# First sublayer's modulation on one core: its weights loaded ahead of x, its rows transposed tile by tile

## The chip, the cores and the metric

The program runs on one core of a Trainium2 chip. The metric is device time in microseconds (us) of one execution; the kernel before has 2074.36 us, the median of 3 runs.

## The reference, cut to what matters

The network takes x (256 rows of 1024, fp32) through two sublayers with stick-breaking attention or retention, each followed by a sublayer with a mixture of experts, and then through a second block. The change touches what stands ahead of attention (i = 0) and of retention (i = 1):

```python
def adaln_params(c, w, b):
    m = jax.nn.silu(c) @ w + b
    shift, scale, gate = jnp.split(m, 3, axis=-1)
    return shift[:, None, :], scale[:, None, :], gate[:, None, :]

for i in range(DEPTH):
    shift, scale, gate = adaln_params(c, ada_w[i, 0], ada_b[i, 0])
    h = x * (1.0 + scale) + shift
    y = stick_breaking_attention(h, sb_w_in) if i == 0 else retention(h, positions, ret_w_in, ...)
    x = layer_norm(DEEPNORM_ALPHA * x + (1.0 + gate) * y, ln_g[i, 0], ln_b[i, 0])
    ...                     # the mixture-of-experts sublayer
```

Here `ada_w[i, 0]` is 1024 x 3072, so shift, scale and gate need 4 MB of weights each.

## The kernel before, in words

Rows of x lie in two tiles of 128 (t = 0, 1), columns in eight blocks of 128 (k = 0 to 7). Every fp32 matrix is split into a high and a low part (`split`, L148: ScalarE casts the high part, L151, VectorE subtracts it for the low part, L153 or in four pieces L160), and a product is three matmuls (`mm3`).

**Shift, scale, gate.** `ada_all` (L232) is a generator. It calls `ada_rows` (L206) for shift, scale and gate in turn; each loads four chunks of 1 MB (L217, "w<-ada_w" in the profile) and multiplies each with the repeated silu(c) in 8 matmuls of 32 x 256 (L163, "y<-w,c_rep", two records apiece in the trace). It yields behind each chunk, so that a chunk is issued where the caller asks for the next one. After scale, `ada_cols` (L241) turns the two rows into columns sc and sh, which the modulation needs; the gate comes later, its chunks between those of the projections.

**Modulation.** `modulated` (L370) wants h transposed: for each k, `transposed` (L357) takes a bank of PSUM, transposes the block of both tiles into it (L187), and calls `each`: one engine, VectorE for even k (L379), ScalarE for odd k (L377), evicts it with scale and shift into a tile t2, and `split` makes the high and low part, "a" in the profile. `modulated` runs twice: ahead of attention (source x) and of retention (source the output of the layer norm).

**Projections.** `proj_t` and `proj_n` multiply h with 256 columns of weights, 1 MB, loaded by `wload` (L385; L392 is its DMA) and split into two tiles "hl": 48 matmuls of 128 x 256 for a projection. Attention has 12 of them (sb_w_in), retention 24 (ret_w_in).

**Order.** `block1` (L1717) sets the program order: silu(c), the load of x, the constants (`consts1`), then the generators. The order on each engine is then made by a scheduler that simulates a timeline; within an `issue_after` block an instruction must come behind a named one of its engine. Pools bound what can be under way: 6 tiles w and 6 tiles hl for weights, 4 banks ps for products and transposes, 4 banks y for accumulators. All the large loads go through SP's one queue, in its order; an SP instruction that waits for a free tile holds those behind it.

Of the kernel before, what the change touches and what calls it, by code (L numbers as in the profile page):

```python
# [8 lines left out]
F32 = mybir.dt.float32  # L9
# [5 lines left out]
AF = mybir.ActivationFunctionType  # L15
# [4 lines left out]
P = 128  # L20
S = 256
T = 2
D = 1024
KB = 8
# [30 lines left out]
class Net:  # L55
    def __init__(self, ctx, tc, io, dbg=None):
        self.ctx, self.tc, self.nc, self.io = ctx, tc, tc.nc, io
        self.dbg = dbg or {}
        self.flip = self.pieces = self.wide = 0
        self.left, self.early, self.done = [], {}, {}  # L60

    def phase(self, name):
# [136 lines left out]
    def ada_init(self):  # L199
        nc = self.nc  # L200
        sc = self.cst.tile([P, KB], F32, name="c_silu")
        nc.scalar.activation(sc, self.c_col, AF.Silu)
        self.crep = self.cst.tile([P, KB, 32], F32, name="c_rep")
        nc.vector.tensor_copy(self.crep, sc[:, :, None].to_broadcast([P, KB, 32]))

    def ada_rows(self, i, j, slot, out):  # L206

        nc = self.nc
        W = self.io["ada_w"][i, j].rearrange("(k p) n -> p k n", p=P)
        if slot == 2:  # L210
            bias = self.wk.tile([P, 256], F32, name="ada_b", bufs=1)
            nc.gpsimd.dma_start(bias, self.io["ada_gate_b"][i * 2 + j])
        pm = self.acc.tile([P, 512], F32, name="y")[:, :256]
        for k2 in range(4):
            w = self.hl(F32) if self.wide > k2 % 3 else self.w()
            w = w.rearrange("p (k n) -> p k n", k=2)
            nc.sync.dma_start(w, W[:, k2 * 2:k2 * 2 + 2, slot * D:(slot + 1) * D])  # L217
            for k in range(2):
                kk = k2 * 2 + k
                for c in range(4):  # L220
                    self.mm(pm[32 * c:32 * c + 32], self.crep[:, kk, :],
                            w[:, k, c * 256:(c + 1) * 256], kk == 0, kk == 7)
            if k2 < 3:
                yield
        if slot == 2:
            nc.vector.tensor_tensor(out, pm, bias, op=OP.add)
        else:
            nc.vector.tensor_copy(out, pm)
# [75 lines left out]
    def layer_norm(self, x, y, i, j):  # L304
# [32 lines left out]
            self.left = [(t, s, x, grow, brow) for t in range(T) for s in (slice(0, 512), slice(512, D))]  # L337
        return xh

    def behind(self):  # L340

        return self.tc.issue_after(next(i for i in reversed(self.nc.cur_bb.bb.instructions)
                                        if i.engine == self.vector))
# [25 lines left out]
    def modulated(self, src, sc, sh):  # L369
        nc = self.nc  # L370
        hi, lo = (self.act8(F32R).rearrange("p (k s) -> p k s", k=KB) for _ in range(2))
        self.pieces = PC[0]

        def each(k, pt):
            f = self.t2(S)
            if k % 2:
                nc.scalar.activation(f, pt, AF.Identity, scale=sc[:, k:k + 1], bias=sh[:, k:k + 1])  # L377
            else:
                nc.vector.tensor_scalar(f, pt, sc[:, k:k + 1], sh[:, k:k + 1], op0=OP.mult, op1=OP.add)  # L379
            self.split(hi[:, k], lo[:, k], f)  # L380
        self.transposed(src, each)
        return hi, lo


# [1306 lines left out]
def consts1(net):  # L1691
    nc = net.nc
    k1 = net.load_const("pack1")
    pick(k1, PACK1, net)
    for n, v in (("nones", -1.0), ("ones", 1.0)):
        t = net.cst.tile([P, P], F32, name="c_" + n)
        nc.gpsimd.memset(t, v)
        setattr(net, n, t)
    net.zerob = net.cst.tile([P, P], BF, name="c_zerob")
    nc.gpsimd.memset(net.zerob, 0.0)  # L1700
    net.identb = net.cst.tile([P, P], BF, name="c_identb")
    nc.gpsimd.tensor_copy(net.identb, net.ident)
    net.maskb = net.cst.tile([P, P], BF, name="c_maskb")
    nc.gpsimd.tensor_scalar(net.maskb, net.stri, BIG, -BIG, op0=OP.mult, op1=OP.add)
# [13 lines left out]
def block1(net, s5=True):  # L1718
    nc = net.nc
    net.xm = net.side_pool("xm")  # L1720
    x = net.x_mid = net.xm.__enter__().tile([P, T, D], F32, name="x_mid")
    with ExitStack() as ctx:
        net.open_stream(ctx, 6, 6, 5, 6, 8, "1")
        net.phase("start")
        net.ada_init()
        nc.sync.dma_start(x, net.io["x"].rearrange("(t p) d -> p t d", p=P))
        consts1(net)
        prev = {(0, 0): None}
        for i, j in ((0, 1), (1, 0), (1, 1)):
            q = i * 2 + j - 1  # L1730
            prev[i, j] = net.lng[:, q], net.lnb[:, q]
        ada = {ij: net.ada_all(*ij, prev[ij]) for ij in prev}

        def without_gate(ij):
            while ij not in net.mod:
                yield next(ada[ij])
        net.early[0] = [net.io["ret_w_in"][0]]
        net.jobs += [ada[0, 0]] + [net.s5_params()] * s5 + [ada[0, 1], without_gate((1, 0))]
        s5 = [net.s5_tables()] * s5
        while (0, 0) not in net.mod:  # L1740
            net.background()
        src = x
        for i in range(2):
            for j in range(2):
                net.phase(f"sub{i}{j}")
                net.rate = 1
                if (i, j) == (0, 1):
                    net.rope_tables()
                if (i, j) == (1, 0):
                    net.jobs += [[ada[1, 0], ada[1, 1]] + s5, [ada[1, 0]] + s5 + [ada[1, 1]], [ada[1, 1]] + s5 + [ada[1, 0]], s5 + [ada[1, 0], ada[1, 1]]][GO]  # L1750
                sc, sh, m2 = net.mod[i, j]
                if j == 0:
                    hx = net.modulated(src, sc, sh)
                    y = net.stick(hx) if i == 0 else net.retention(hx, src)
                else:
                    y = net.moe(i, src, sc, sh)
                net.phase(f"ln{i}{j}")
                while net.jobs:
                    net.background()
                if j == 0:  # L1760
                    net.router(*net.mod[i, 1][:2])
                src = net.layer_norm(x, y, i, j)
                net.dump(f"x{i}{j}", x)
# [92 lines left out]
@with_exitstack  # L1856
def whole(ctx, tc, io):
    net = Net(ctx, tc, io)
    net.open_main(ctx)
    block1(net)  # L1860
    block2(net, io["out"])
# [16 lines left out]
```

## Time and profile before

| what | value |
|---|---|
| runs | 2067.89, 2074.36, 2075.95 us; median 2074.36 |
| profiled execution | 2072.57 us, its span 2070.8 us |
| PE (matmul) busy | 1958.4 us, 95% of the span |
| VectorE (DVE) busy | 1206.9 us, 58% |
| ScalarE (ACT) busy | 802.1 us, 39% |
| GpSimd (POOL) busy | 410.5 us, 20% |
| moved by DMA | 496.09 MB, mean 240 GB/s |

A share of busy time is a mean over stages with different limits. Attention lies at about 34 to 200 us of the span, the first mixture of experts at 205 to 456, retention at 470 to 665, and so on. A time with an interval in a row is a start and a length in us; "<-" in brackets names what ended the wait ahead of it.

### The profile page before, as it was taken

The numbers are of one execution on the slowest core, as the hardware profiler recorded it, in microseconds if no ns is written. First come the engines' busy times: TensorE is split into PE (matmuls) and PEld (weight loads), VectorE is DVE, ScalarE is ACT, GpSimd is POOL, SyncE is SP. The second block draws the span as 40 slices with busy tenths as digits, with TensorE's granted clock in tenths as the row PEclk, the third lists the DMA queues.
The fourth block names the chain that finished last, engine by engine and source line by source line (L and its number), as shares of the span: only waits on it lengthen the run. The fifth ranks groups of instructions, "written<-read, shape, count | busy, mean of one in ns | idle before, by whom it ended". The sixth has DMA issues, their size and how long they took to land.

```text
span 2070.8 us, 31874 instructions
## 1 busy us (share of the span) xinstructions
PE 1958.4 (95%) x12566; PEld 1527.3 (74%) x12567; DVE 1206.9 (58%) x2489; ACT 802.1 (39%) x1254; POOL 410.5 (20%) x319
## 2 busy tenths in 40 slices
PE   6999999989999999987988999999999999999998
PEld 4967543438898844434766889999999998888886
DVE  3554321129895422104687569767999986555555
ACT  3344111124454311113433553555444445444444
POOL 1000000002232000000231134544665550000000
PEclk9999899999999999998998999999999999999999
DMA  9797699998875699996332361544564446555564
GB/s 388 284 405 269 253 393 394 394 390 284 304 271 187 245 365 394 395 391 263 138 116 88 114 257 32 163 143 143 163 194 154 145 151 193 193 194 193 194 194 151
DMA packets 155887, 496.09 MB, mean 240 GB/s; under 512 B 10176, under 2 KB 10592, under 8 KB 147152
## 3 DMA queue, kind: packets, MB, share of 16 engines
q1 hardware_dynamic: 152880, 483.42, 65.1%
q0 software_dynamic: 2848, 10.53, 1.4%
q8 instruction: 102, 1.67, 0.3%
q14 instruction: 57, 0.47, 0.1%
HBM read 486.30 MB, written 7.61 MB: 239 GB/s over the span
## 4 chain that ended last, share of the span: by engine, by line
PE 72%; DVE 10%; ACT 2%; issue 2%; DMA 2%; POOL 1%; POOLq 0%; SPq 0%; DVEq 0%; ACTq 0%
PE ps L163 42%; PE y L163 28%; DMA w<-moe_w_down 1%; DVE pair L1553 1%; PE y L1206 1%; DVE i L1454 1%; PE ps L187 1%; DVE et L1477 1%; DVE hl L153 1%; DVE pos L1465 1%; DVE v L1453 1%; ACT hl L151 0%; DMA raw<-s_tab 0%; DVE big L1561 0%; DVE cand L1460 0%
## 5 line engine op out<-in xcount | busy, mean ns | idle before, releaser
L163 PE MATMUL ps<-hn,pair 128*128 128x256 f32 x3072 | 383.5, 285 | 4.2 <-DVE pair L1553 4.1
L163 PEld LDWEIGHTS ps<-hn,pair 128*128 128x128 f32 x3072 | 373.8, 192 | 5.6 <-DVE pair L1553 5.1
L163 PE MATMUL y<-pair,hn 128*128 128x512 f32 x1512 | 342.9, 389 | 0.0
L163 PEld LDWEIGHTS y<-pair,hn 128*128 128x128 f32 x1512 | 283.8, 188 | 59.0
L163 PE MATMUL ps<-w,t 128*64 128x512 f32 x624 | 277.3, 595 | 8.7 <-DMA w<-moe_w_down 2.8
L163 PE MATMUL ps<-hl,t 128*64 128x512 f32 x624 | 278.4, 596 | 4.5 <-DVE t L194 3.1
L1553 POOL TENSOR_TENSOR pair<-raw,pair 128x640 fp32r<-128x640 f32 x128 | 235.2, 1845 | 158.0 <-ACT pair L1551 151.8
L153 DVE TENSOR_TENSOR pair<-raw,pair 128x1024 fp32r<-128x1024 f32 x128 | 156.7, 1225 | 147.1 <-ACT pair L151 147.1
L151 ACT CAST hl<-w 128x2048 fp32r<-128x2048 f32 x79 | 150.2, 1903 | 136.6 <-PE ps L163 77.1
L151 ACT CAST pair<-raw 128x1024 fp32r<-128x1024 f32 x128 | 135.0, 1055 | 172.7 <-PE y L163 171.6
L163 PEld LDWEIGHTS ps<-w,t 128*64 128x64 f32 x624 | 81.6, 137 | 117.2 <-issue 103.8
L1551 ACT CAST pair<-raw 128x1024 fp32r<-128x1024 f32 x128 | 134.2, 1051 | 65.7 <-PE ps L163 23.9
L153 DVE TENSOR_TENSOR hl<-w,hl 128x2048 fp32r<-128x2048 f32 x51 | 119.2, 2337 | 54.2 <-ACT hl L151 51.1
L163 PE MATMUL ps<-hl,a 128*128 128x256 f32 x1008 | 129.7, 287 | 1.8 <-ACT hl L151 1.8
L163 PEld LDWEIGHTS ps<-hl,t 128*64 128x64 f32 x624 | 81.1, 137 | 67.6 <-issue 60.7
L163 PEld LDWEIGHTS ps<-hl,a 128*128 128x128 f32 x1008 | 123.9, 191 | 5.7 <-ACT hl L151 2.0
L330 POOL TENSOR_TENSOR ln_st<-ln_st,c_mhalf 128x1 f32<-128x1 f32 x8 | 6.1, 768 | 605.3 <-ACT ln_st L327 605.2
L731 DVE TENSOR_TENSOR t<-t,ps 128x512 f32<-128x512 f32 x16 | 11.0, 688 | 171.8 <-PE ps L163 171.8
L163 PE MATMUL ps<-a,hl 128*128 128x256 f32 x864 | 105.7, 284 | 1.2 <-DVE a L153 1.2
L163 PEld LDWEIGHTS ps<-a,hl 128*128 128x128 f32 x864 | 104.2, 192 | 2.6 <-DVE a L153 1.4
L163 PE MATMUL ps<-a,t 128*64 128x512 f32 (+1 forms) x352 | 100.2, 537 | 1.4 <-ACT t L196 1.4
L747 DVE SCALAR_TENSOR_TENSOR t<-ps,m_sw,t 128x512 fp32r<-128x512 f32 x32 | 24.0, 750 | 132.5 <-ACT t L746 132.0
(431 smaller groups left out, 2886.5 us busy)
## 6 DMA issues: line engine op xcount, KB each, us to landing
raw<-peer_u SPq DMA_DIRECT2D x128, 512.0 KB, 3.4
raw<-peer_v SPq DMA_DIRECT2D x128, 512.0 KB, 3.4
w<-ada_w SPq DMA_DIRECT2D x35, 1024.0 KB, 7.5
w<-moe_w_down SPq DMA_DIRECT2D x28, 1024.0 KB, 14.3
hl<-moe_w_down SPq DMA_DIRECT2D x28, 1024.0 KB, 14.2
w<-moe_w_up SPq DMA_DIRECT2D x26, 1024.0 KB, 14.2
hl<-moe_w_up SPq DMA_DIRECT2D x26, 1024.0 KB, 14.3
w<-moe_w_gate SPq DMA_DIRECT2D x24, 1024.0 KB, 14.7
```

The lines of the kernel that those rows point to most:

```text
L151: nc.scalar.copy(hi, src)
L153: nc.vector.tensor_tensor(lo, src, hi.bitcast(F32), op=OP.subtract)
L163: self.last_mm = self.nc.tensor.matmul(out, lhsT=lhsT, rhs=rhs, start=start, stop=stop, skip_group_check=True)
L187: self.nc.tensor.transpose(out, in_, self.ident[:in_.shape[0], :in_.shape[0]])
L747: V.scalar_tensor_tensor(yl[hf], py, sw, yh[hf].bitcast(F32), op0=OP.mult, op1=OP.subtract)
L1206: self.nc.tensor.matmul(py[32 * q:32 * q + 32, :S], lhsT=self.s5_ct[ct][:, 4 * i + q], rhs=ab[q % 2][:, x, ri], start=j == 0, stop=j == 3, ...
L1453: V.max(v[:, a, rs], s)
L1454: V.max_index(ix[:, a, rs], v[:, a, rs], s)
L1465: V.max_index(pos[:, 2, rs], top[:, h, rs], cd)
L1477: V.tensor_reduce(et[:, 0:2, h], oh.rearrange("p a k j -> p a j k"), axis=AX.X, op=OP.add)
L1551: nc.scalar.copy(up[:, 0], ur)
L1553: lo = eng.tensor_tensor(up[:, 1, ks], ur[:, ks], up[:, 0, ks].bitcast(F32), op=OP.subtract)
```

## The change

Two things. In `block1`, the generator for shift and scale of the first sublayer runs ahead of everything else: its first six chunks are issued, then x, then the last two chunks, then the constants. Those last two chunks take tiles of the hl pool (`self.ahead`), not of w. In `modulated`, which both places use, four banks are taken with two blocks k each; all transposes are written out tile by tile (all k of t = 0, then all of t = 1), and only then the eight calls of `each`, in each of which the instructions of VectorE and ScalarE must come behind the last ones of the call before (`in_order`).

```diff
@@ ada_rows
-            w = self.hl(F32) if self.wide > k2 % 3 else self.w()
+            w = self.hl(F32) if self.wide > k2 % 3 or self.ahead and slot == 1 and k2 > 1 else self.w()
@@
+    def in_order(self):
+
+        stack = ExitStack()
+        for eng in (self.vector, self.scalar):
+            stack.enter_context(self.tc.issue_after(next(i for i in reversed(self.nc.cur_bb.bb.instructions)
+                                                         if i.engine == eng)))
+        return stack
@@ modulated
-        self.transposed(src, each)
+        pts = [self.psum((P, 2, S)) for _ in range(KB // 2)]
+        for t in range(T):
+            for k in range(KB):
+                self.transpose(pts[k // 2][:, k % 2, t * P:t * P + P], src[:, t, k * P:k * P + P])
+        for k in range(KB):
+            with self.in_order() if k else nullcontext():
+                each(k, pts[k // 2][:, k % 2])
@@ block1
-        nc.sync.dma_start(x, net.io["x"].rearrange("(t p) d -> p t d", p=P))
+
+        net.ahead = 1
+        first = net.ada_all(0, 0, None)
+        for n in range(8):
+            if n == 6:
+                nc.sync.dma_start(x, net.io["x"].rearrange("(t p) d -> p t d", p=P))
+            next(first)
+        net.ahead = 0
         consts1(net)
-        prev = {(0, 0): None}
+        prev = {}
...
-        ada = {ij: net.ada_all(*ij, prev[ij]) for ij in prev}
+        ada = {(0, 0): first, **{ij: net.ada_all(*ij, prev[ij]) for ij in prev}}
```

The instructions stand as follows at three places. First, SP's queue at the program's start, before:

```order
L78 DMA c_pack_66<-pack 128x224
L1726 DMA x_mid<-x 128x2x1024
L217 DMA w<-ada_w 128x2x1024 x8
L392 DMA w<-sb_w_in 128x2048
L217 DMA w<-ada_w 128x2x1024
```

and now:

```order
L78 DMA c_pack_66<-pack 128x224
L217 DMA w<-ada_w 128x2x1024 x6
L1745 DMA x_mid<-x 128x2x1024
L217 DMA hl<-ada_w 128x2x1024 x2
L406 DMA w<-sb_w_in 128x2048
```

x has moved behind six of the eight chunks; what stands behind the eighth chunk is the same as before.

Second, ScalarE at the first modulation (t2 is an evicted block, a its high part, "hl<-w" the cast of a whole chunk of projection weights), before:

```order
L377 ACTIVATE t2_229<-ps_226,ada_sh_214,ada_sc_213 128x256
L151 CAST hl_281<-w_280 128x2048
L377 ACTIVATE t2_243<-ps_240,ada_sh_214,ada_sc_213 128x256
L151 CAST a_217<-t2_222 128x256
L151 CAST a_217<-t2_229 128x256
L151 CAST a_217<-t2_236 128x256
L377 ACTIVATE t2_257<-ps_254,ada_sh_214,ada_sc_213 128x256
L151 CAST a_217<-t2_250 128x256
L151 CAST a_217<-t2_264 128x256
L377 ACTIVATE t2_271<-ps_268,ada_sh_214,ada_sc_213 128x256
L151 CAST a_217<-t2_243 128x256
L151 CAST a_217<-t2_257 128x256
```

and now (w_276, w_350 and w_424 are the weights of the first three projections):

```order
L151 CAST hl_277<-w_276 128x2048
L151 CAST a_217<-t2_239 128x256
L385 ACTIVATE t2_243<-ps_219,ada_sh_202,ada_sc_201 128x256
L151 CAST a_217<-t2_243 128x256
L151 CAST a_217<-t2_247 128x256
L385 ACTIVATE t2_251<-ps_220,ada_sh_202,ada_sc_201 128x256
L151 CAST hl_351<-w_350 128x2048
L151 CAST a_217<-t2_251 128x256
L151 CAST hl_425<-w_424 128x2048
L151 CAST a_217<-t2_255 128x256
L385 ACTIVATE t2_259<-ps_221,ada_sh_202,ada_sc_201 128x256
L151 CAST a_217<-t2_259 128x256
```

The first chunk's cast has moved ahead of all blocks, and the casts of the second and third chunk have moved in front of blocks 3 and 4; before, both stood behind block 7. VectorE has the low parts of the second and third chunk at the same places between the blocks.

Third, VectorE at the second modulation, ahead of retention (L153 writes a low part), before:

```order
L379 TENSOR_SCALAR t2_3428<-ps_3425,ada_sc_1593,ada_sh_1594 128x256
L379 TENSOR_SCALAR t2_3442<-ps_3439,ada_sc_1593,ada_sh_1594 128x256
L379 TENSOR_SCALAR t2_3456<-ps_3453,ada_sc_1593,ada_sh_1594 128x256
L153 TENSOR_TENSOR a_3424<-t2_3428,a_3423 128x256
L379 TENSOR_SCALAR t2_3470<-ps_3467,ada_sc_1593,ada_sh_1594 128x256
L153 TENSOR_TENSOR a_3424<-t2_3435,a_3423 128x256
L153 TENSOR_TENSOR a_3424<-t2_3442,a_3423 128x256
```

and now:

```order
L387 TENSOR_SCALAR t2_3441<-ps_3421,ada_sc_1589,ada_sh_1590 128x256
L153 TENSOR_TENSOR a_3420<-t2_3441,a_3419 128x256
L153 TENSOR_TENSOR a_3420<-t2_3445,a_3419 128x256
L387 TENSOR_SCALAR t2_3449<-ps_3422,ada_sc_1589,ada_sh_1590 128x256
L153 TENSOR_TENSOR a_3420<-t2_3449,a_3419 128x256
L153 TENSOR_TENSOR a_3420<-t2_3453,a_3419 128x256
L387 TENSOR_SCALAR t2_3457<-ps_3423,ada_sc_1589,ada_sh_1590 128x256
L153 TENSOR_TENSOR a_3420<-t2_3457,a_3419 128x256
L153 TENSOR_TENSOR a_3420<-t2_3461,a_3419 128x256
L387 TENSOR_SCALAR t2_3465<-ps_3424,ada_sc_1589,ada_sh_1590 128x256
```

Before, three evictions stood ahead of the first low part; now each eviction of VectorE stands behind the low parts of the two blocks before it.

## Rows read from the trace of the kernel before

**Rows 1.** Windows: busy us by engine (count), granted PE clock, DMA share, GB/s.

```profile
60.00:105.00 45.00, 45.00 (x408) 42.80 (x407) 26.43 (x36) 16.05 (x20) 2.17 (x4) 1.00 0.73 267
300.00:350.00 50.00, 48.47 (x232) 20.03 (x229) 8.08 (x20) 7.02 (x15) 0.00 (x0) 1.00 1.04 396
550.00:600.00 50.00, 50.00 (x419) 46.56 (x419) 47.19 (x81) 27.31 (x40) 14.51 (x18) 1.00 0.84 293
```

**Rows 2.** The page's chain of work that ended last, share by engine.

```profile
PE 72%; DVE 10%; ACT 2%; issue 2%; DMA 2%; POOL 1%; POOLq 0%; SPq 0%; DVEq 0%; ACTq 0%
```

**Rows 3.** Timeline of SP's queue: start and length of two issues, us.

```profile
13.15 0.37 SPq L217 DMA_DIRECT2D w<-ada_w  x1
...
29.40 0.34 SPq L392 DMA_DIRECT2D w<-sb_w_in  x1
```

**Rows 4.** DMA issues, the same two in that order; last number: us to landing.

```profile
w<-ada_w SPq DMA_DIRECT2D x1, 1024.0 KB, 14.2
...
w<-sb_w_in SPq DMA_DIRECT2D x1, 1024.0 KB, 13.1
```

**Rows 5.** Timeline of PE, 23 to 52 us.

```profile
23.88 1.07 PE L163 MATMUL y<-w,c_rep 128*32 128x256 f32 x16 [0.54 <-DMA w<-ada_w]
27.41 1.93 PE L163 MATMUL y<-w,c_rep 128*32 128x256 f32 x16 [2.46 <-DMA w<-ada_w]
29.93 1.94 PE L163 MATMUL y<-w,c_rep 128*32 128x256 f32 x16 [0.59 <-DMA w<-ada_w]
...
39.46 11.53 PE L163 MATMUL ps<-a,hl 128*128 128x256 f32 x94 [1.17 <-DVE a L153]
50.92 1.07 PE L163 MATMUL y<-w,c_rep 128*32 128x256 f32 x16
51.92 6.01 PE L163 MATMUL ps<-hl,a 128*128 128x256 f32 x48
```

**Rows 6.** Timeline of ACT, 34 to 42 us.

```profile
34.47 1.89 ACT L151 CAST hl<-w 128x2048 fp32r<-128x2048 f32 x1
36.26 0.57 ACT L377 ACTIVATE t<-ps,ada_sh,ada_sc 128x256 f32<-128x256 f32 x1
36.72 1.01 ACT L151 CAST a<-t 128x256 fp32r<-128x256 f32 x3
...
40.07 1.91 ACT L151 CAST hl<-w 128x2048 fp32r<-128x2048 f32 x1
```

**Rows 7.** Timeline of DVE, 33 to 42 us.

```profile
33.95 0.99 DVE L379 TENSOR_SCALAR t<-ps,ada_sc,ada_sh 128x256 f32<-128x256 f32 x2
...
36.59 2.49 DVE L160 TENSOR_TENSOR hl<-w,hl 128x512 fp32r<-128x512 f32 x4
38.99 2.76 DVE L153 TENSOR_TENSOR a<-t,a 128x256 fp32r<-128x256 f32 x8
```

**Rows 8.** Timeline of DVE at the second modulation.

```profile
468.18 1.62 DVE L379 TENSOR_SCALAR t<-ps,ada_sc,ada_sh 128x256 f32<-128x256 f32 x3 [0.43 <-PE ps L187]
...
472.84 0.42 DVE L153 TENSOR_TENSOR a<-t,a 128x256 fp32r<-128x256 f32 x1 [0.24 <-ACT a L151]
473.18 4.90 DVE L160 TENSOR_TENSOR hl<-w,hl 128x512 fp32r<-128x512 f32 x8
```

**Rows 9.** Timeline of PE at the second modulation.

```profile
467.80 0.77 PE L187 MATMUL ps<-c_pack,a 128*128 128x128 f32 x5 [0.56 <-DVE a L335]
...
469.59 1.07 PE L163 MATMUL y<-w,c_rep 128*32 128x256 f32 x16
...
470.79 23.28 PE L163 MATMUL ps<-a,hl 128*128 128x256 f32 x192
```

**Rows 10.** Windows of 2 us at the first modulation, columns as in rows 1.

```profile
26.00:28.00 2.00, 0.59 (x8) 0.36 (x12) 0.73 (x7) 0.00 (x0) 1.95 (x2) 0.73 1.04 416
34.00:36.00 2.00, 1.96 (x9) 1.38 (x9) 1.48 (x3) 1.99 (x2) 0.00 (x0) 0.50 0.99 410
```

More of the change, by code (lines that the diff above doesn't have):

```diff
@@ L58, in __init__ @@
         self.dbg = dbg or {}
-        self.flip = self.pieces = self.wide = 0
+        self.flip = self.pieces = self.wide = self.ahead = 0
         self.left, self.early, self.done = [], {}, {}
@@ L201, in ada_init @@
         sc = self.cst.tile([P, KB], F32, name="c_silu")
-        nc.scalar.activation(sc, self.c_col, AF.Silu)
+        self.scalar = nc.scalar.activation(sc, self.c_col, AF.Silu).ins.engine
         self.crep = self.cst.tile([P, KB, 32], F32, name="c_rep")
```

## The prediction, made before the changed kernel ran

> **What bounds the kernel now.** I read the busy time by stages first. Away from the expert stages PE is the limit: it is busy for all of 60 to 105 us and all of 550 to 600, at full clock [rows 1], and the chain that ended last lies on PE for 72% of the span [rows 2]. The expert stages run at 396 GB/s with the DMA engines occupied [rows 1]; their weights go into tiles that earlier work frees, so a shift ahead of them shifts them too. So what the change does at each of its two places counts by one measure: when does PE reach the same point of its own work, and how much of the interleaved gate work has it done by then?
>
> Next the start, in the order DMA, PE, ScalarE, VectorE. PE's waits there end on landings: a chunk's matmuls start at 23.88, the seventh's at 27.41, the eighth's at 29.93 [rows 5]. The seventh was issued at 13.15 and took 14.2 us to land; the third projection's weights were issued at 29.40 and took 13.1 [rows 3, 4], to 42.5. For 1 MB that is a queue of several transfers, always fed, one landing about every 2.5 us. Last the modulation: VectorE evicts the first block at 33.95 and writes low parts from 38.99, behind its low part of the first weights [rows 7]; ScalarE's cast of those weights stands in the middle of the blocks [rows 6]; PE runs the first two projections from 39.46 without a gap and starts the third at 51.92 [rows 5].
>
> **The change, part by part.**
>
> *The queue at the start.* Nothing is added or taken away: x and eight chunks are 9 MB in either order, and behind them SP's list is the same. The first six chunks land one transfer earlier, x about six later; neither is what the modulation waits for, since the eighth chunk ends it. Its landing can move only if the two waits for a free w tile (the seventh chunk's issue at 13.15 [rows 3]) cost something. From 23.88 to 27.41 are 3.53 us, where 2.52 follow [rows 5]: at most 1.0 us too much. Bounds for every landing behind it: 0 to 1.0 us earlier. I take 0, as the seventh chunk was queued long before its turn came.
>
> *The transposes.* Twelve of the 16 now run ahead of sc and sh, against 6 before. What is saved behind sc and sh is up to six transposes of 2.71 / 10 = 0.27 us, but PE is not what is late there (below), so: nothing, covered by the wait for ScalarE and VectorE. If that cover were gone it would be a gain of 1.6 us at most; I leave it out.
>
> *The order within the first modulation.* This is the large term. ScalarE's list now has the cast of the third projection's weights in front of the high part of block 4, and VectorE's list has their low part in front of the low part of block 4. Those weights land at 42.5 (above). From there: cast 1.9 [rows 6] to 44.4; low part of the weights 2.5 [rows 7] to 46.9; low parts of blocks 4 and 5 at 2.76 / 8 = 0.345 [rows 7] to 47.6; eviction of block 6 at 0.54 to 48.1 (1.62 / 3 [rows 8]); high part 6 at 1.01 / 3 = 0.34, eviction 7 at 0.57, high part 7 at 0.34 [rows 6] to 49.4; low part 7 to 49.75. PE's list has 34 matmuls of the first two projections behind that, at 11.53 / 94 = 0.123 us [rows 5], 4.2 us, and half a gate chunk, 0.5: the third projection starts at 54.45, against 51.92 before, 2.5 later. But by then PE has done 3.5 gate chunks instead of 2, and one is worth 1.0 us (50.92 to 51.92 [rows 5]): 1.5 back. **Net +1.0 us.** Bounds: -1.0 if everything lands 1.0 earlier and the order of the two engines costs another 1.0 less than I add up; +5.2 if the last 34 matmuls run at half clock (below).
>
> A rule bears on this term. The row first: VectorE's low parts of the blocks start at 38.99, right at the end of the weights' low part of 36.59 [rows 7], though the first high part was there at about 37.1 [rows 6]. Nothing passed. The Trainium skill states it ("PSUM — Partial Sum Buffer", Engine vs sequencer instructions): the queues of ScalarE and VectorE are strictly first in, first out. By the rule the waiting cast holds blocks 4 to 7, as in my sum; without it the blocks would be done by about 44 and the third projection would start some 4 us before my 54.45, a gain. The trace agrees with the rule, in the one row named.
>
> *The order within the second modulation.* No weights' cast stands between the blocks here, but the two engines now go in lockstep, two blocks to a round: eviction 0.54 on VectorE, high part 0.34, eviction 0.57, high part 0.34 on ScalarE, low part 0.42 [rows 8], with the hand-overs (some 0.05 each) 2.3 us. Four rounds from about 468.3 end at 477.6; two further VectorE instructions, which stood later before, are now ahead of the last low part and add 0.5: 478.1, against 473.26 before (472.84 + 0.42 [rows 8]). PE needs the last block only for the last 4 matmuls of the first projection, 0.5: done at 478.6. Before, the first 48 of 192 matmuls from 470.79 at 23.28 / 192 = 0.121 [rows 9] were done at 476.6: 2.0 later now, with one gate chunk more done, 1.0. **Net +1.0 us.** Bounds: -1.1, if the lockstep hides behind PE altogether, since PE can start on block 0 at 469.7 instead of 470.79; +4.8, if the whole delay of the last low part shows.
>
> *The rest.* The scheduler also puts retention's background work and parts of the expert loops in another order, with the same instructions. PE is full there (50.00 of 50.00 us [rows 1]), so I take 0.
>
> **Sum.** 2072.57 for the profiled execution, plus 1.0 and 1.0: 2074.6. The median of the runs, 2074.36, lies 1.8 above that execution, and the runs span 8 us. I predict **2076 us**, no difference that a measurement of this kernel can tell: it can tell about 0.5%, 10.4 us.
>
> **Rivals.**
>
> *Slower: a low clock behind the first modulation.* The place is PE's last 34 matmuls there. For: the granted clock falls from full to 0.73 of it in 26 to 28 us, when PE was busy for 0.59 of 2 us, and is 0.50, the lower level of 1.2 GHz, in 34 to 36 [rows 10]. In the changed order PE waits for single blocks between 41 and 50 us as it waited for single chunks then. At the lower level 34 matmuls take another 4.2 us: 2074.4 + 2.0 + 4.2, or 2080.6. The Trainium skill ("TensorE: Matmul & The Clock Gate", What's actually happening) says that the throttled state is the default and that activity releases it. Rows 10 agree with that. Against: some 19 matmuls and a gate chunk lie between the blocks and keep PE going for much of the time. It decides from a granted clock below 0.75 in 44 to 54 us.
>
> *Slower: VectorE in retention.* VectorE begins retention's splits up to 4.8 us later, and at 47.19 of 50 us busy [rows 1] it regains that only slowly. If its lead of some 4 us over PE was all that kept PE full, projections wait for low parts, up to the two splits of 4.9 us at 473.18 [rows 8]: 2081.3. Against: PE's own 2.0 us are part of the same delay.
>
> *Faster: the queue and the lockstep both cost nothing.* All landings 1.0 earlier (place one at 0.0), PE starting at 469.7 in place two (-1.1), and the transposes' 1.6 showing: -2.7 on the median, 2071.7. For: the 3.53 us between two chunks [rows 5], and PE's list interleaves blocks of two projections. Against: the queue behind is byte for byte the same.
>
> *Other places decide.* The new order of background work in retention: one split of weights missed is 1.9 + 2.5 us [rows 6, 7]: 2078.8 + 2.0, about 2081. With PE full, a gain is hardly there to be had.
>
> **How the numbers follow.** Forecast 0.45, with 2072 to 2080 as its own range: 2.0 with some 2 to 4 either way, from the bounds. Low clock 0.15, VectorE in retention 0.1, faster 0.2, other places 0.1. The range reaches above to both slower rivals and the other places with 2 us of the runs' spread, below to the faster rival with half that spread: 2068 to 2083. Faster by over 0.5% (below 2064) has no case, only what I overlook: 0.03. Slower by over 0.5% (above 2084.7) needs both slower rivals at once (2085.5): 0.06. The rest, 0.91.
>
> **What the profile would show.** Right: PE's third projection starts at 53.5 to 55.5 with 3.5 gate chunks done; ScalarE idles up to 1.5 us ahead of the third cast, waiting on a load of w; the last low part of the second modulation ends at 477 to 479, counted from the same start of its evictions; attention's end is about 1 us late, retention's about 2. Wrong: weights of the third projection landing by 40; a third projection before 52; a granted clock of 0.5 in 44 to 54; gaps of PE in retention that end on VectorE; or a stage behind retention that differs by more than 2 us.

## The result: slower by about half a percent, and the profile after

The changed kernel takes 2082.36 us (median of 7 runs, 2078.84 to 2088.04); the kernel before, run beside it, 2071.05 us (median of 7, 2067.89 to 2075.95). The ratio is 1.0057, with a 95% interval of 1.0039 to 1.0075. That is small, but it is a loss: no run of the one reaches a run of the other. The time lies at the upper edge of the range given (2068 to 2083) and 6 us above the forecast of 2076. The profiled execution of the change took 2085.07 us, its span is 2083.3 us, 12.5 us more than before.

The page shows almost nothing of it. Its head and its chain, which answer to [rows 2]:

```profile
span 2083.3 us, 31881 instructions
...
PE 1969.3 (95%) x12566; PEld 1537.1 (74%) x12567; DVE 1207.6 (58%) x2489; ACT 802.5 (39%) x1254; POOL 412.3 (20%) x319
...
PE 72%; DVE 9%; DMA 3%; ACT 2%; issue 2%; POOL 1%; POOLq 0%; DVEq 0%; ACTq 0%; SPq 0%
...
PE ps L163 42%; PE y L163 28%; DMA w<-moe_w_down 1%; DMA s_tab<-a 1%; PE y L1220 1%; DVE pair L1567 1%; PE ps L187 1%; DVE et L1491 1%; ACT hl L151 1%; DVE i L1468 1%; DVE hl L153 1%; DVE pos L1479 0%; DVE v L1467 0%; DVE ps L1213 0%; POOL hl L160 0%
```

One item is new: the transfer `s_tab<-a` is now on the chain. To find the rest, the same pieces of work were looked up in both traces, and how much later each begins after the change (us):

| landmark | before | after | later by | added since the line above |
|---|---|---|---|---|
| third projection, first matmul | 51.92 | 55.86 | 3.94 | 3.94 |
| layer norm behind attention, first scaling | 195.91 | 198.24 | 2.33 | -1.61 (gate chunks done early) |
| second modulation, first eviction | 468.18 | 470.19 | 2.01 | -0.32 |
| retention, first matmul of the output projection | 650.14 | 657.45 | 7.31 | **5.30** |
| layer norm behind retention, first scaling | 698.69 | 707.59 | 8.90 | 1.59 |
| second expert stage, first matmul | 722.51 | 734.88 | 12.37 | 3.47 |
| end | 2070.8 | 2083.3 | 12.5 | 0.1 |

**The first modulation.** PE's timeline of the change, columns as in [rows 5]:

```profile
36.04 1.94 PE L163 MATMUL y<-w,c_rep 128*32 128x256 f32 x16
37.91 3.06 PE L163 MATMUL ps<-a,hl 128*128 128x256 f32 x17
...
43.72 0.74 PE L163 MATMUL ps<-a,hl 128*128 128x256 f32 x4 [1.06 <-DVE a L153]
45.07 2.27 PE L163 MATMUL ps<-a,hl 128*128 128x256 f32 x15 [0.61 <-ACT a L151]
47.27 1.07 PE L163 MATMUL y<-w,c_rep 128*32 128x256 f32 x16
48.27 7.09 PE L163 MATMUL ps<-a,hl 128*128 128x256 f32 x57
55.29 0.64 PE L163 MATMUL y<-w,c_rep 128*32 128x256 f32 x8
```

And ScalarE's and VectorE's, which answer to [rows 6, 7]:

```profile
38.91 1.89 ACT L151 CAST hl<-w 128x2048 fp32r<-128x2048 f32 x1
40.69 0.41 ACT L151 CAST a<-t 128x256 fp32r<-128x256 f32 x1
42.81 1.90 ACT L151 CAST hl<-w 128x2048 fp32r<-128x2048 f32 x1 [1.72 <-DMA w<-sb_w_in]
44.62 0.40 ACT L151 CAST a<-t 128x256 fp32r<-128x256 f32 x1
```
```profile
44.75 2.50 DVE L160 TENSOR_TENSOR hl<-w,hl 128x512 fp32r<-128x512 f32 x4 [0.62 <-ACT hl L151]
47.16 0.76 DVE L153 TENSOR_TENSOR a<-t,a 128x256 fp32r<-128x256 f32 x2
...
49.75 0.43 DVE L153 TENSOR_TENSOR a<-t,a 128x256 fp32r<-128x256 f32 x1 [0.48 <-ACT a L151]
```

What these lines show: the cast of the third projection's weights at 42.81 waits for its landing, with blocks 4 to 7 behind it in ScalarE's list; the low part of those weights, at 44.75, has blocks behind it in VectorE's; and PE waits for single blocks at 43.72 and 45.07 and still has 57 matmuls to do from 48.27.

**Retention.** From its first eviction to its output projection it took 181.96 us and now 187.26. Most of that is one place. First SP's queue of the change, then of the kernel before (start and length of the issues):

```profile
608.53 8.93 SPq L449 DMA_DIRECT2D w<-ret_w_out  x4
617.54 0.42 SPq L1159 DMA_DIRECT2D s_tab<-a  x1
```
```profile
605.85 7.65 SPq L435 DMA_DIRECT2D w<-ret_w_out  x3
613.60 0.42 SPq L1145 DMA_DIRECT2D s_tab<-a  x1
621.22 21.70 SPq L435 DMA_DIRECT2D w<-ret_w_out  x5
```

ScalarE and PE of the change behind it:

```profile
621.75 0.37 ACT L961 ACTIVATE t<-ps 128x256 f32<-128x256 f32 x1
627.33 0.63 ACT L905 ACTIVATE a<-a 128x512 f32<-128x512 f32 x1 [5.21 <-DMA s_tab<-a]
627.86 0.61 ACT L906 ACTIVATE a<-a 128x512 f32<-128x512 f32 x1
628.38 1.88 ACT L151 CAST hl<-w 128x2048 fp32r<-128x2048 f32 x1
630.17 0.64 ACT L955 COPY t<-ps 128x256 f32<-128x256 f32 x2
```
```profile
620.43 5.99 PE L163 MATMUL ps<-hl,a 128*128 128x256 f32 x48
630.58 2.08 PE L163 MATMUL ps<-t,t 128*128 128x256 f32 x4 [4.17 <-ACT t L955]
```

The background work of retention computes eight tables in one tile (`s5_tables`) and stores each to memory. The seventh table's store is issued behind four loads of output weights; it lands 9.70 us later, at 627.24 (the chain of waits has it as `617.54 9.70 DMA s_tab<-a`). The eighth table's first instruction, L905, may not overwrite the tile until then. In ScalarE's list the copies L955, the evictions that PE waits for, stand behind it, and behind a cast of weights. PE is idle for 4.17 us. In the kernel before, the store behind three loads at 613.60 is the last one, and no table waits for it.

In these traces a wait of ScalarE for a store need not cost PE anything. The kernel before has one too:

```profile
533.15 0.63 ACT L891 ACTIVATE a<-a 128x512 f32<-128x512 f32 x1 [3.73 <-DMA s_tab<-a]
```

PE waits for nothing there. The change has another of 5.65 us, until 542.24, and PE loses 0.18 us behind it, at 543.70. At 627.33, in contrast, PE had been idle since its 48 matmuls ended at 626.42.

**Low clock.** Windows of the change by the granted clock, columns as in [rows 1] with PE alone; then the kernel before at the router:

```profile
630.00:632.00 2.00, 1.42 (x3) 0.54 0.03 12
632.00:634.00 2.00, 2.00 (x11) 0.61 0.52 35
634.00:636.00 2.00, 2.00 (x17) 1.00 0.65 199
656.00:658.00 2.00, 1.04 (x5) 0.87 0.43 138
658.00:660.00 2.00, 2.00 (x6) 0.50 0.77 217
660.00:662.00 2.00, 2.00 (x8) 0.78 0.78 302
706.00:712.00 6.00, 5.69 (x36) 0.72 1.05 388
712.00:718.00 6.00, 6.00 (x27) 0.50 1.04 402
718.00:724.00 6.00, 5.72 (x26) 0.50 0.76 273
```
```profile
700.00:706.00 6.00, 5.24 (x42) 1.00 1.05 391
706.00:712.00 6.00, 5.72 (x27) 0.51 1.02 401
```

Behind PE's wait the clock is at its lower level, 1.2 GHz, for some 4 us; again at 658 to 660, where 12 matmuls of the output projection take 4.61 us instead of 3.02 (the 1.59 of the table); and in the router (the 3.47). There the short matmuls ran at half for about 10 us of the stretch before, from 706 on, and now for about 20, from 709 on. So 5.06 of the 12.5 us arose behind retention, in stretches at the lower clock; why the clock is low there in the change is not shown.

### The profile page after: what moved, and what is told of

Same layout as the page of the kernel before. It is cut to its first block, busy times and chain, and to the rows that moved or that the text cites. A ratio compares the mean times of both kernels' runs of the same rounds, so it can differ in the third digit from the quotient of the medians.

```text
span 2083.3 us, 31881 instructions
## 1 busy us (share of the span) xinstructions
PE 1969.3 (95%) x12566; PEld 1537.1 (74%) x12567; DVE 1207.6 (58%) x2489; ACT 802.5 (39%) x1254; POOL 412.3 (20%) x319
## 4 chain that ended last, share of the span: by engine, by line
PE 72%; DVE 9%; DMA 3%; ACT 2%; issue 2%; POOL 1%; POOLq 0%; DVEq 0%; ACTq 0%; SPq 0%
PE ps L163 42%; PE y L163 28%; DMA w<-moe_w_down 1%; DMA s_tab<-a 1%; PE y L1220 1%; DVE pair L1567 1%; PE ps L187 1%; DVE et L1491 1%; ACT hl L151 1%; DVE i L1468 1%; DVE hl L153 1%; DVE pos L1479 0%; DVE v L1467 0%; DVE ps L1213 0%; POOL hl L160 0%
## 5 line engine op out<-in xcount | busy, mean ns | idle before, releaser
L163 PE MATMUL ps<-hn,pair 128*128 128x256 f32 x3072 | 383.4, 285 | 4.5 <-DVE pair L1567 4.4
L163 PEld LDWEIGHTS ps<-hn,pair 128*128 128x128 f32 x3072 | 373.8, 191 | 5.7 <-DVE pair L1567 5.2
L163 PE MATMUL y<-pair,hn 128*128 128x512 f32 x1512 | 342.9, 389 | 0.0
L163 PEld LDWEIGHTS y<-pair,hn 128*128 128x128 f32 x1512 | 283.9, 188 | 58.9
L163 PE MATMUL ps<-w,t 128*64 128x512 f32 x624 | 277.2, 595 | 7.9 <-ACT t L196 2.7
L163 PE MATMUL ps<-hl,t 128*64 128x512 f32 x624 | 278.1, 596 | 4.5 <-DVE t L194 3.1
L153 DVE TENSOR_TENSOR pair<-raw,pair 128x1024 fp32r<-128x1024 f32 x128 | 156.8, 1225 | 147.0 <-ACT pair L151 147.0
L151 ACT CAST hl<-w 128x2048 fp32r<-128x2048 f32 x79 | 150.2, 1903 | 148.1 <-PE ps L163 79.6
L151 ACT CAST pair<-raw 128x1024 fp32r<-128x1024 f32 x128 | 135.0, 1055 | 172.6 <-PE y L163 171.3
L163 PEld LDWEIGHTS ps<-w,t 128*64 128x64 f32 x624 | 81.6, 137 | 116.1 <-issue 104.8
L153 DVE TENSOR_TENSOR hl<-w,hl 128x2048 fp32r<-128x2048 f32 x51 | 119.2, 2338 | 55.4 <-ACT hl L151 52.3
L163 PE MATMUL ps<-hl,a 128*128 128x256 f32 x1008 | 130.4, 287 | 1.8 <-ACT hl L151 1.8
L163 PEld LDWEIGHTS ps<-hl,t 128*64 128x64 f32 x624 | 81.2, 137 | 66.6 <-issue 59.9
L163 PEld LDWEIGHTS ps<-hl,a 128*128 128x128 f32 x1008 | 124.6, 192 | 5.0 <-ACT hl L151 2.0
L163 PE MATMUL ps<-a,hl 128*128 128x256 f32 x864 | 109.8, 286 | 2.9 <-ACT a L151 1.2
L163 PEld LDWEIGHTS ps<-a,hl 128*128 128x128 f32 x864 | 105.8, 193 | 8.7 <-DVE a L153 3.2
L163 PE MATMUL ps<-a,t 128*64 128x512 f32 (+1 forms) x352 | 100.2, 537 | 1.4 <-ACT t L196 1.4
```

The lines of the kernel that those rows point to most:

```text
L151: nc.scalar.copy(hi, src)
L153: nc.vector.tensor_tensor(lo, src, hi.bitcast(F32), op=OP.subtract)
L163: self.last_mm = self.nc.tensor.matmul(out, lhsT=lhsT, rhs=rhs, start=start, stop=stop, skip_group_check=True)
```

## The experiments

Theory A, as first put: most of the loss is the late store of a table. Theory B: the delay of the modulations is handed on, with the low clock. The first four runs take the change apart. In the runs that keep `name_ph` line numbers are 1 to 4 higher than in the change (L164 is its L163, L959 its L955, L993 its L989).

**Loads alone** (the old modulation at both places):

```
-        pts = [self.psum((P, 2, S)) for _ in range(KB // 2)]
...
+        self.transposed(src, each)
         return hi, lo
```

> The change's order of loads with the old modulation at both places. Theory A (the late store: most of the loss is one store of s5 tables in retention that SP issues behind a fourth load of the output projection's weights): SP's order in retention is the one before, so no wait of PE near 620 to 630 and the time of the kernel before, within 2 us either way. Theory B (the delay of the modulations and of the start is handed on, and the low clock with it): also near the time before, since the modulations are the old ones; 0 to 1 us earlier if the earlier chunks help. Third projection at 51 to 52.5 us by both. A third outcome, over 3 us slower, would put the loss on the load order itself.

Measured: 2071.3 us against 2072.95, ratio 0.9990 (0.9981 to 0.9998). The third projection starts at 50.62, a little ahead of what was expected; retention takes 181.96 us from its first eviction to its output projection, to the hundredth what it took before, and PE waits there for nothing. So the loads cost nothing. The small gain was not that of earlier landings: the eighth chunk's matmuls start at 29.90, as in [rows 5]. The scheduler put VectorE's low part of the first weights at 34.33 instead of 36.59 [rows 7], between the blocks, and PE runs the projections from 37.75 without a gap instead of from 39.46.

**New modulation only in front of retention** (the phase's name is kept in `name_ph`):

```
+        if self.name_ph == 'sub00':
+            self.transposed(src, each)
+            return hi, lo
         pts = [self.psum((P, 2, S)) for _ in range(KB // 2)]
```

> The new modulation only in front of retention; the first one is the old one, the loads stand in the new order. Theory A: SP's list in retention is that of the full change, so PE waits 3 to 6 us near 615 to 630 for ScalarE, which waits for the store; with the stretches of low clock behind it 5 to 11 us slower than before. Theory B: the first modulation's 2.3 us are gone and the second costs 0 to 1: within 2 us of the time before.

Measured: 2084.37 us, ratio 1.0053 (1.0037 to 1.0069). The layer norm behind attention begins at 195.78, where it did before; retention takes 189.13 us, with PE's wait for the copies at 627.68, 4.08 us. The first place isn't needed for the loss. Theory B falls here.

**New modulation only in the first place:**

```
+        if self.name_ph == 'sub10':
+            self.transposed(src, each)
+            return hi, lo
         pts = [self.psum((P, 2, S)) for _ in range(KB // 2)]
```

> The new modulation only in the first place; in front of retention the old one. Theory A: the first place costs 2.3 us at the third projection (55 to 56 us instead of 51.9), no table store that ScalarE waits for stands behind loads of the output weights: 2 to 4 us slower than before. Theory B: the same 2.3 us and stretches of low clock on top where the program is shifted: 6 to 10 us slower.

Measured: 2081.68 us, ratio 1.0044 (1.0031 to 1.0058): more than theory A gave, and within the 6 to 10 us of theory B. But the trace doesn't have B's cause: behind retention the router took 20.83 us, 3 less than before. The layer norm behind attention is 2.4 later, as expected; and the scheduler gave retention yet another order, in which it takes 188.95 us although its modulation is the old one. What PE waited for there (us in total, times, longest):

```profile
PE ps L164 <- DVE t L993: 3.4, 2, 3.2
PE ps L164 <- ACT hl L152: 2.0, 1, 2.0
PE ps L164 <- ACT t L959: 1.1, 1, 1.1
```

ScalarE waited 5.59 and 5.00 us for stores of tables, until 531.8 and 557.5; the second was issued behind three loads of input weights, and PE's 2.0 us, until 563.42, follow on it. The longest wait does not come from a store: it ended at 529.35, ahead of the first landing, on VectorE's product with the decay (L993), which stands behind the low part of a chunk of weights. So late stores aren't bound to one place, and they are not the only cost of a new order.

**The stores on ScalarE's own queue** in the full change:

```
-            nc.sync.dma_start(self.s5_tab[pr // 2], tab)
+            nc.scalar.dma_start(self.s5_tab[pr // 2], tab)
```

> The full change, but the eight table stores are issued on ScalarE's queue, directly behind the instruction that writes the table, and no longer stand in SP's list. Theory A: the wait of ScalarE of 5.2 us for the store shrinks to 2 us or less and PE's gap of 4.2 us near 626 goes: 2 to 5 us slower than before, 6 to 9 faster than the change. Theory B: PE's gap near 626 may go but the time stays 8 us or more above that of before.

Measured: 2079.38 us, ratio 1.0039 (1.0024 to 1.0053): 6.4 us slower by the medians and 8.1 by the ratio, more than theory A gave and, by the ratio, at the lower edge of theory B. ScalarE and PE at the same place:

```profile
618.30 0.35 ACTq L1159 DMA_DIRECT2D s_tab<-a  x1
...
623.92 0.63 ACT L905 ACTIVATE a<-a 128x512 f32<-128x512 f32 x1
...
628.00 1.90 ACT L151 CAST hl<-w 128x2048 fp32r<-128x2048 f32 x1 [2.93 <-PE ps L163]
629.81 0.64 ACT L955 COPY t<-ps 128x256 f32<-128x256 f32 x2
```
```profile
630.23 1.13 PE L163 MATMUL ps<-t,t 128*128 128x256 f32 x4 [2.14 <-ACT t L955]
```

The store, issued at 618.30, has let the next table start at 623.92; no wait for it is left. PE's gap is 2.14 instead of 4.17. So the store made 2.0 us of it, and the other 2.14 are a second cost: the cast L151 stands in front of the two copies, and it waits until PE has finished the projection whose weights it overwrites. Theory A became: what costs is the *order* that the scheduler gave retention's background work, the stores being one of its forms, and the constraint `in_order` is what moved it. Theory C, against it: the new transposes and shared banks delay the blocks by themselves.

**Without the constraint**, first in the first place alone (the old modulation in front of retention), then at both:

```
-            with self.in_order() if k else nullcontext():
+            with nullcontext():
```

> The change's loads; in the first place the new transposes and banks but without the constraint that keeps the blocks' instructions in order; the old modulation in front of retention. Theory A (the constraint and what the scheduler makes of it: the weights' third cast in front of block 4, and another order of retention's background work): the cast stands behind all blocks again, the third projection starts at 50 to 51.5 us, retention has the order of before and no wait of PE above 1 us but the one of 0.96 at its output; 3 us faster to 0 us against before. Theory C (the new transposes and the shared banks themselves delay the blocks): third projection at 53 us or later, 2 us slower or more.

Measured: 2074.44 us, ratio 1.0002 (0.9992 to 1.0011). ScalarE has cast all eight blocks by 39.1 us, ahead of the second and third weights; retention takes 181.97 us, with no wait. The third projection begins at 53.45, late against what was expected and past the 53 us of theory C. That is the clock's doing: it was at its lower level (0.50) from 36 to 42 us, and the 94 matmuls ahead took 13.65 us, where they took 11.53 in [rows 5] at full clock.

> The full change without the constraint, at both places. Theory A: third projection at 50 to 51.5 us; in retention the last table store stands behind three loads of output weights with no table behind it, so no wait for it; waits of PE there together below 1.5 us beside the 0.96; 3 us faster to 3 us slower than before. Theory C: 6 us slower or more, as the change.

Measured: 2076.71 us, ratio 1.0017 (1.0005 to 1.0030). Third projection at 52.02, past the 51.5 expected; retention 183.69 us, with one wait of PE of 3.10 us on VectorE's product with the decay (L989), twice what was expected. Theory C's price falls with both: the transposes and banks are the change's, and most of the loss is gone. What is left at both places, 0.17% with an interval that leaves 1 out, comes without the constraint.

**Two background steps earlier** in the full change:

```
                 if j == 0:
+                    net.background(2 * i)
                     hx = net.modulated(src, sc, sh)
```

> The full change with two steps of background work called ahead of the second modulation, so that in retention the store behind four loads of output weights is the last one, with no table behind it that waits for it. Theory A: ScalarE's wait of 5.2 us for a store near 622 to 627 is gone or below 2 us, PE's gap there is at most 2.2 us (the cast that stands in front of the copies); 4 to 8 us slower than before, 3 to 7 faster than the change. Theory C: 10 us or more slower than before, since the modulations are the change's.

Measured: 2076.3 us, ratio 1.0020 (1.0009 to 1.0031). The constraint is still in place here; only the order of the background work is another. At the place in question PE waits 2.14 us, as in the run with the stores moved; retention takes 185.82, less than the change's 187.26 but with other waits of 1.8 and 1.7 us. The run won more than that: from the layer norm to the first expert matmul it took 20.68 us, the change 27.29.

**The same edit, one step, in the kernel before**, with nothing of the change in it:

> The kernel before, nothing of the change in it, with one step of background work called ahead of the second modulation; it puts two table stores behind two and three loads of output weights in SP's list, each with a table behind it. Theory A: PE waits 2 to 5 us in the second half of retention for ScalarE, which waits for a store; 2 to 7 us slower than before. Theory C: the modulations are the old ones, so the time is that of before within 1.5 us.

Measured: 2084.62 us, ratio 1.0053 (1.0035 to 1.0071): the whole loss of the change, from one step of background work called earlier. The size was underrated and the place missed. PE in the first half of retention:

```profile
530.77 2.41 PE L163 MATMUL ps<-t,t 128*128 128x256 f32 x6 [3.24 <-DVE t L975]
...
549.23 1.22 PE L163 MATMUL ps<-t,t 128*128 128x256 f32 x2 [3.18 <-ACT t L941]
```

and ScalarE at the second of these:

```profile
545.98 1.90 ACT L151 CAST hl<-w 128x2048 fp32r<-128x2048 f32 x1 [4.22 <-PE ps L163]
547.78 0.62 ACT L891 ACTIVATE a<-a 128x512 f32<-128x512 f32 x1
548.31 0.61 ACT L892 ACTIVATE a<-a 128x512 f32<-128x512 f32 x1
548.83 0.62 ACT L941 COPY t<-ps 128x256 f32<-128x256 f32 x2
```

The copies that PE waits for stand behind a cast and two instructions of a table. No store is waited for here; the order alone does it. ScalarE's two waits for a store in this retention, 2.85 us until 559.67 and 3.09 until 620.93, are followed by no wait of PE.

**Constraint on ScalarE alone**, in the first place alone (the old modulation in front of retention):

```
-        for eng in (self.vector, self.scalar):
+        for eng in (self.scalar,):
```

> New transposes in the first place with the constraint on ScalarE alone (VectorE's instructions are free), the old modulation in front of retention, the change's loads. ScalarE's cast of the third projection's weights stands in front of block 6 instead of block 4; retention's background work has the order of before. Theory A (two separate costs, the first place's constraint and retention's order): third projection at 52.5 to 55 us, no wait of PE above 1 us in retention but the 0.96 at its output, 0 to 4 us slower than before. Theory C (one constraint in the first place is enough to cost what the change costs): 7 us slower or more.

Measured: 2071.35 us, ratio 0.9991 (0.9983 to 1.0000). Third projection at 51.78, earlier than expected, retention 181.97 us without a wait. The cast does not stand where it was expected, in front of block 6, but behind all eight blocks:

```profile
41.78 0.41 ACT L152 CAST a<-t 128x256 fp32r<-128x256 f32 x1
42.47 1.91 ACT L152 CAST hl<-w 128x2048 fp32r<-128x2048 f32 x1 [0.28 <-DMA w<-sb_w_in]
```

The first line is the high part of the last block, the second the cast of the third projection's weights. With the blocks ahead of that cast, the first place costs nothing. (The second projection's weights still stand between the blocks, in front of the high part of block 5.)

**The change, the loads alone and the kernel before once more.**

> The change itself once more, to see which pieces of its 12.5 us come again in another execution. Theory A: the third projection at 55.5 to 57.5 us and PE's wait of 4.2 us near 627 come again, and ev2 to the output projection of retention takes 186 to 189 us; the stretch of low clock in the router behind retention (3.5 us) moves or is missing. Theory D (the low clock is the cause): the stretch of low clock comes again at the same work, with the same 3.5 us.

Measured: 2082.6 us, ratio 1.0043 (1.0030 to 1.0056). Third projection at 56.12, PE's wait 4.39 us at 631.62, retention 187.35: as expected. But the router's low clock came again too: from the layer norm to the first expert matmul both executions of the change took 27.29 us, where the other twelve traces took 20.7 to 25.0. Here theory A's expectation failed, and the sign of a theory D came, that the low clock is the cause. All fourteen traces have the clock low somewhere in this stretch: for about 20 us in both executions of the change, for 3 to 14 in the others, and in the kernel before for about 10 in one execution and 3 in the other. The long one is missing in the run with the new modulation only in front of retention (23.53), whose stores and output weights stand in SP's list as in the change, so the order in retention isn't enough for it; and as that run loses 0.53%, D isn't the whole cause. Why the long stretch comes isn't shown.

> The change's loads with the old modulation at both places once more, as the version that may beat both kernels. If its gain is real: ratio to before below 1 again with an interval that leaves 1 out, 0.9975 to 0.9998. If it was chance: an interval that holds 1.

Measured: 2070.01 us against 2073.86, ratio 0.9990 (0.9980 to 1.0001). The same value as the first time, with an interval that just holds 1, the sign named for chance; so a gain over the kernel before is not shown. Loads alone are the version to keep: some 2 us faster than before, if anything, and by the medians 11 to 12.6 faster than the change.

> The kernel before once more, one look, for how far its stages move from one execution to another. Expected: third projection at 50.5 to 53.5 us, retention from its first eviction to its output projection 181 to 183 us with no wait of PE above 1 us but the 0.96; the stretch from the end of retention to the first expert matmul 22 to 27 us by where the clock is low.

Measured: 2073.07 us in its one run; third projection at 52.35, retention 183.00 us with no wait beside those it had before, 22.6 us from the layer norm to the expert matmul. All within what was expected.

Retention in all runs, beside what PE waited for inside it (the waits on the transposes of L187, 1.2 to 1.4 us in every trace, are left out):

| kernel | retention, us | PE's waits, us | ratio to before |
|---|---|---|---|
| before; loads alone (twice); first place free; ScalarE alone | 181.96 to 181.97 | 0 | 1; 0.9990; 1.0002; 0.9991 |
| before once more | 183.00 | 0 | |
| both places free | 183.69 | 3.1 | 1.0017 |
| stores on ScalarE's queue | 185.70 | 3.4 | 1.0039 |
| two steps earlier | 185.82 | 6.2 | 1.0020 |
| the change (twice) | 187.26, 187.35 | 5.2, 5.4 | 1.0057, 1.0043 |
| first place alone | 188.95 | 6.6 | 1.0044 |
| second place alone | 189.13 | 6.3 | 1.0053 |
| before, one step earlier | 192.54 | 8.9 | 1.0053 |

Every kernel whose retention has no new wait runs as fast as before, and every other one is slower. The last digits of the ratios don't follow the waits: other stages of single executions moved by some 4 us either way (in "second place alone" the way from the second expert stage to the end took 7.4 us more), and that is not explained.

## Why the prediction was right or wrong

**Queue at the start: right.** Taken as 0. The seventh and eighth chunks' matmuls start at 27.45 and 30.01, against 27.41 and 29.93 [rows 5].

**Transposes: right.** Taken as 0, covered by ScalarE and VectorE, and that cover is what PE waits for at 43.72 and 45.07.

**First modulation: the wait right, the path behind it wrong, the term too small.** +1.0 forecast; 2.33 at the layer norm behind attention, 2.39 to 3.78 in the other runs with the full constraint in the first place. The weights had landed by 42.8 (42.5 forecast), the cast waited with the blocks behind it, and 3.5 gate chunks were done, all as forecast. The start of the third projection was not: 55.86 instead of 54.45. The forecast let PE's last 34 matmuls wait for the last low part, which ended at 50.18 (49.75 forecast). PE never waited for it. At one in 7.09 / 57 = 0.124 us it still had 41 or 42 matmuls to do at 50.18 and came to the last 34 only at 51.12. What held it were two waits ahead, for block 3 at 43.72, behind the low part of the second projection's weights (at 40.83 in VectorE's list), which the forecast left out, and for block 4 at 45.07, behind the waiting cast. From there PE runs without a gap, 72 matmuls and a chunk and a half of gate work, to 55.86. The Trainium skill's rule ("PSUM — Partial Sum Buffer", Engine vs sequencer instructions) that ScalarE and VectorE take their queues strictly in order decided rightly here: the trace agrees, with the high part of block 4 at 44.62 right behind the cast that waited 1.72 us.

**Second modulation: 1 us too much.** +1.0 forecast. The lockstep came as forecast: the last low part ended 10.15 us after the start of the evictions (9.8 forecast). From there to the second pair of projections, 561.48 before and 564.43 after, the change loses only 0.94 us, with 1.03 us of waits in that stretch, 0.64 of them on the background's order and not on the modulation (0.46 at 527.19, 0.18 at 543.70). So most of the lockstep hides behind PE, toward my lower bound.

**The rest: the step that failed.** "PE is full there (50.00 of 50.00 us), so I take 0." It measured 5.30 us in retention, of which the second modulation holds at most 0.94, then 1.59 at its output projection and 3.47 in the router. The last two came at the lower clock, for which no cause is shown. That PE was full in [rows 1] said that in the old order every copy and low part came in time. It said nothing of a new order of the same instructions. The order of retention's stores and loads in SP's list, and of casts and copies in ScalarE's, was there to be read ahead of the run, and I didn't read it.

**The rivals.** "Other places decide" named retention's background work and gave about 2081, near the 2082.36 measured, with a chance of 0.1; its mechanism, a missed split of weights, was only half of it (the cast ahead of the copies, 2.14), the late store the other half (2.0). "VectorE in retention" gave 2081.3; PE's long wait in the change ends on ScalarE, so that rival was wrong by its own sign, though longer waits on VectorE came in other orders (3.24 us in the kernel before, one step earlier). "Low clock behind the first modulation" did not come: the granted clock of the change in 44 to 54 us was 1.00; in one other run (two steps earlier) it was 0.54 in 46 to 48 and cost some 1.5. "Faster" did not come. Of the signs named for being wrong one came: a stage behind retention that differs by more than 2 us, the router.

**No difference: wrong, and the range held by luck.** The measured 0.57% lies above even the 0.5% that the forecast took as the least that can be told; seven runs told it with an interval from 0.39 on. The range held the time because it reached to the slower rivals, and because the kernel before came out at 2071.05 us in seven runs, 3.3 below the 2074.36 it was built on. Over 2074.36 the range allowed a rise of 8.6 us; the rise was 11.3.

## What to carry to other kernels

A busy share of 100% shows that the order at hand works, and nothing about the next order. Where an edit makes a scheduler reorder a stage, compare the lists of that stage on every in-order queue and look for two things: a store whose tile is rewritten next, behind loads that are many and large, and a cast that waits for PE in front of the copies that PE waits for. An ordering constraint in one place can cost more elsewhere: in the first place alone it cost 2.4 us there and 7.0 in retention. Try the same edit without it, and try each part alone, since here one part (the loads) was worth keeping and the other was not.

## What the runs showed of the hardware that was not expected

A 512 KB store issued on SP's queue at 617.54, behind three 1 MB loads that had not landed yet, took 9.70 us to land. Issued on ScalarE's queue at 618.30, with two such loads under way and the next one issued behind it, it took 5.54. The Trainium skill ("DMA: Bandwidth & Descriptors", Rules for kernel authors) says that transfers spread over the issuing engines gain no bandwidth, since all run on the same DMA engines and interleave. No run here measures that. Of the 4.16 us that the one small transfer landed sooner, the runs don't show how much is the other queue and how much the one load less ahead of it.

The same 94 matmuls of the first projections, in the same order and from nearly the same start, took 11.53 us in one execution [rows 5] and 13.23 in the run "before, one step earlier", whose program is the same up to there; the granted clock was 0.50 in 40 to 42 us in the latter and 1.00 in the former. So a difference of 1.7 us between two single traces at this place can be the clock alone. After each of the long waits of PE in retention (2.0 to 4.4 us) the clock was low for some 3 to 7 us. In the change, 15 matmuls took 2.80 us behind the wait at 630.58, where 24 took 3.22 at 616.80. The Trainium skill ("TensorE: Matmul & The Clock Gate", What's actually happening) has the throttled state as the default that activity releases; the trace agrees, with 0.54 and 0.61 in the two windows behind the wait and 1.00 after. The long low stretch in the change's router, about 20 of 27.29 us in both executions, stays open.
